# One instruction order for TensorE through a recurrence: products, chain stages and a clock of delays

## The chip, the cores and the metric

The kernel runs on one core of a Trainium2 chip. The metric is the device time of one execution in microseconds (us). Before the change it is 2061.61 us, the median of three runs (2059.32 to 2065.57).

## The reference, cut to what matters

Two layers of a diffusion backbone work on 256 context tokens and 512 latent tokens of width 1024, in float32. The even layer, which comes first, has two token mixers side by side: four mLSTM heads and eight RWKV-7 heads. Their outputs are joined and projected back, and a squared-ReLU MLP of width 4096 follows. The odd layer has RG-LRU and neighbourhood attention in the same places. Context tokens pass through the even layer too, since the odd layer's latent tokens read them.

The change concerns the RWKV-7 mixer. Each head keeps a 64 x 64 state S. Every token decays it, corrects it by a rank-one term and adds another:

```python
def step(S, inp):
    r_t, w_t, k_t, v_t, a_t, b_t = inp
    sa = jnp.einsum('zbhij,zbhj->zbhi', S, a_t)
    S = S * w_t[..., None, :] + sa[..., :, None] * b_t[..., None, :] + v_t[..., :, None] * k_t[..., None, :]
    return S, jnp.einsum('zbhij,zbhj->zbhi', S, r_t)
```

It runs forwards and backwards over the context (256 tokens) and goes on from there over the latent tokens (512). The output is the latent stream after a last normalization.

## The kernel before, in words

**Products.** A float32 product with a weight matrix is made of three products of a rounded type: weight and input are each split into a high and a low part (`split_w` L228 for weights: ScalarE rounds, VectorE or GpSimd subtracts; `split_x` L279 for inputs), and `gemm_w` (L254) sums high x high, high x low and low x high in one PSUM bank. A product of 8 blocks has 24 matmuls, of 512 columns for latent tokens and of 256 for context tokens. Two PSUM banks (`psg`) take turns.

**The recurrence in chunks.** The RWKV scan is cut into 12 steps of 64 tokens (4 context, 8 latent); each step treats both directions and all eight heads. `pre(s)` (L839) prepares a step, independently of the state. Its stages: loads from DRAM (`bk`, `ar`, `AS`, `X`); the products `psA` of 64 rows each, one half of the partitions (`q`) after the other, whose results ScalarE and VectorE mask; a way through DRAM to bring the 16 x 16 blocks of a triangular matrix together (`M`); its inversion in 30 small dependent instructions (`tm`, `Xi`), on GpSimd up to step 4 and on VectorE after it; a way back (`Xr`); and four rounds of tiny matmuls (`psI`), each followed by VectorE or ScalarE, that merge the blocks to the inverse `T`. `step(s)` (L949) is the serial part: `pR` (psC<-X,AS), then `pU` (psC<-r,T), then the new state (psC<-X,BK) and the output (psC<-X,Q and psC<-S,ar), with evictions by ScalarE and VectorE between them. Tiles of a step live in one of two sets of buffers, by `s % 2`.

**What runs between.** `fillers` (L1118) yields the other work of this stage piece by piece: `rwkv_in(1)` (L689), which makes the RWKV inputs of the latent tokens from 15 products and many small operations; half of the output projection for the latent tokens (`lat_mlstm` L1031) and for the context (`ctx_mlstm` L1044); then, when step 3 is done, the other half for the context (`ctx_half` L1058) and the context's whole MLP. `pull` (L1077) takes pieces by their estimated length, and the main loop (L1133) gives `step(s)`, `pre(s+1)` and 21 us of fillers in turn; 33 us of fillers (`PL`) are given ahead of step 0. Steps from 4 on need `rwkv_in(1)` and `lat_mlstm`.

**What sets the order.** The program gives instructions in this order, but each engine's final order is made by a scheduler that simulates the program with a model of durations and puts whatever is ready first. All engines, TensorE too, then run their instructions in that fixed order.

`pre(0)` is given earlier, before the last two pieces of the fourth mLSTM head (string in L1089, letter R).

Of the kernel before, what the change touches and what calls it, by code (L numbers as in the profile page):

```python
# [18 lines left out]
P = 128  # L19
D = 1024  # L20
# [97 lines left out]
def hybrid_kernel(ctx: ExitStack, tc: tile.TileContext, A, out):  # L118
# [12 lines left out]

    def mm(o, l, r, start=True, stop=True, shared=False, tile=None):
        kw = {"tile_position": (32 * tile[0], 32 * tile[1])} if tile else {}
        return nc.tensor.matmul(o, l, r, start=start, stop=stop, skip_group_check=shared, **kw)  # L134
# [93 lines left out]
    def split_w(ap, both, pool=None):  # L228

        m = ap.shape[1]  # L230
        n = m if pool else D
        pool = pool or (wide[0] if wcount[0] % 3 == 2 else None) or wp
        wpool = wide[0] if wide[0] is not None and pool is wide[0] else wp
        w = wpool.tile([P, D], F32, tag="w", bufs=3 if wpool is wp else None, name=nm("w"))[:, 0:m]
        nc.sync.dma_start(w, ap)
        wh = pool.tile([P, n], F32R, tag="wh", name=nm("wh"))[:, 0:m]
        nc.scalar.copy(wh, w)  # L237
        wl = pool.tile([P, n], F32R, tag="wl", name=nm("wl"))[:, 0:m]
        wcount[0] += 1
        eng = nc.vector if (2, 0, 3, 1)[wcount[0] % 4] < both else nc.gpsimd  # L240
        eng.tensor_tensor(wl, w, wh.bitcast(F32), op=ALU.subtract)  # L241
        return wh, wl

    def gemm(ap, xs, psp, both=0, k0=0, k1=NK, x0=0):

        w = split_w(ap[:, P * k0:P * k1], both)
        res = [gemm_w(w, x, psp, x0) for x in xs]
# [6 lines left out]
    def gemm_w(w, x, psp, x0=0):  # L254
        (wh, wl), (xh, xl, n) = w, x
        nk = wh.shape[1] // P
        ps = psp.tile([P, n], F32, tag="g", name=nm("psg"))
        for k in range(nk):
# [97 lines left out]
    def mlp(layer, cnd, n, res, FC, psp, side, both, rb, G, stats=None, done=None):  # L356
        us = n / 512 * 5.2
        with ExitStack() as st:
# [12 lines left out]
            for ch in range(DFF // P // FC):  # L371
# [16 lines left out]
                for m in range(NK // 2 if last and done else NK):  # L388
                    add_gated(res[:, m, :], gemm(A["w2"][layer, ch, m], [(hh, hl, n)], psp, both)[0], cnd, m, layer, 5)
# [299 lines left out]
    def rwkv_in(si, psp, psh, tag, last=None):  # L689
# [5 lines left out]
        with tc.tile_pool(name=nm("pha"), bufs=1) as pha, tc.tile_pool(name=nm("ph"), bufs=1) as ph, \  # L695
# [4 lines left out]
            nc.gpsimd.memset(rst[:, ::CR], 0.0)  # L700
            low = [[pha.tile([P, n], F32R, name=nm("low")) for z in range(2)] for kind in range(2)]
# [26 lines left out]
            for p in range(4):  # L728
                gup = ph.tile([P, P], F32, tag="gup", name=nm("gup"))
                nc.sync.dma_start(gup, A["g_up"][:, P * p:P * p + P])  # L730
                kk, k, r = (ph2.tile([P, nch, 64], F32, tag=a, name=nm(a)) for a in ("kk", "k", "r"))
                v = ph.tile([P, nch, 64], F32, tag="v", name=nm("v"))
                inproj(3 + 3 * p, k)
                sq = pha.tile([P, n], F32, tag="zs", bufs=2, name=nm("sq"))
                nc.scalar.activation(c64(sq), k, AF.Square, scale=V["k_k"][:, p:p + 1])
                pst = psh.tile([P, nb, 2], F32, tag=tag, name=nm("pst"))
                for c in range(nb):
# [7 lines left out]
                               rk.rearrange("p c h -> p (c h)")[:, :, None].to_broadcast([P, 2 * nb, 64]))  # L745
                bc = psh.tile([P, nch, 64], F32, tag=tag, name=nm("psbc"))
# [3 lines left out]
                yield us  # L750
                inproj(4 + 3 * p, r)
                q_ = pha.tile([P, nch, 64], F32, tag="zs", bufs=2, name=nm("q"))
                nc.vector.scalar_tensor_tensor(q_, r, V["r_k"][:, p:p + 1], k, op0=ALU.mult, op1=ALU.mult)
                gb = ph.tile([P, 2, n], F32, tag="gb", name=nm("gb"))
                pb = psh.tile([P, nch, 64], F32, tag=tag, name=nm("psb"))
                mm(pb, C["hsum"], q_)
                nc.scalar.copy(c64(gb[:, 1, :]), pb)
                yield us
                inproj(5 + 3 * p, v)
                if p == 3 and last:  # L760
                    last()
                yield us
                th = []
                for z in range(2):
                    up = ph.tile([P, 2, P], F32, tag="up", name=nm("up"))
                    nc.sync.dma_start(up, A["up"][p, z])
                    uh = ph.tile([P, 2, P], F32R, tag="uh", name=nm("uh"))
                    ul = ph.tile([P, 2, P], F32R, tag="ul", name=nm("ul"))
                    nc.scalar.copy(uh, up)
                    nc.gpsimd.tensor_tensor(ul, up, uh.bitcast(F32), op=ALU.subtract)  # L770
                    for kind in range(2):
                        pw = psh.tile([P, nch, 64], F32, tag=tag, name=nm("psw"))
                        mm(fl(pw), uh[:, kind, :], low[kind][z], True, False)
                        mm(fl(pw), ul[hs_[z], kind, :], low[kind][z][hs_[z], :], False, True)
# [3 lines left out]
                        th.append(t_)  # L778
                for z in range(2):
# [24 lines left out]
                    nc.sync.dma_start(bkD[si][:, st, z, p, :], bk)  # L804
                pv = psh.tile([P, nb, P], F32, tag=tag, name=nm("psv"))
                for c in range(nb):
                    nc.tensor.transpose(pv[:, c, :], fl(v)[:, P * c:P * c + P], ident)
                vt = pha.tile([P, nb, P], F32, tag="zs", bufs=2, name=nm("vt"))
                nc.scalar.copy(vt, pv)
                nc.sync.dma_start(vD[si][:, p, :].rearrange("(c t) i -> t c i", t=P), vt)  # L810
                nc.gpsimd.tensor_tensor(c64(gb[:, 1, :]), c64(gb[:, 1, :]), v, op=ALU.mult)
                pg_ = psh.tile([P, n], F32, tag=tag, name=nm("psg"))
# [4 lines left out]
                yield 0.0  # L817
# [21 lines left out]
    def pre(s, X):  # L839
# [3 lines left out]
        pr2 = sets[s % 2]  # L843
        ar = pr2.tile([P, 2, 4, P], F32, tag="ar", name=nm("ar"))
        bk = pr2.tile([P, 2, 4, P], F32, tag="bk", name=nm("bk"))
        Q = pr2.tile([P, 2, 4, 2, 64], F32, tag="Q", name=nm("Q"))
        AS = pr2.tile([P, 2, 4, 2, 64], F32, tag="AS", name=nm("AS"))
        AB = pr2.tile([P, 2, 4, 64], F32, tag="AB", name=nm("AB"))
# [4 lines left out]
        for z in range(2):  # L853
            c = 64 * (ch[z] - s0)
            nc.sync.dma_start(X[64:P, z].rearrange("t p q i -> t (p q i)"), vD[si][c:c + 64].rearrange("t p i -> t (p i)"))
        for z in range(2):
            for q in range(2):
                pa_ = bank("A", [P, 4, P])
                for p in range(4):
                    mm(pa_[:, p, :], bk[hs_[q], z, p, :], ar[hs_[q], z, p, :])  # L860
                nc.scalar.copy(AB[hs_[q], z], pa_[0:64, :, 0:64])
                nc.vector.tensor_tensor(AS[64:P, z, :, q, :], pa_[64:P, :, 0:64], amask(z, 0, HI), op=ALU.mult)
                nc.vector.tensor_tensor(Q[:, z, :, q, :], pa_[:, :, 64:P], amask(z, 1, FULL), op=ALU.mult)
# [8 lines left out]
        M = pr.tile([64, 16, 16], F32, tag="M", name=nm("M"))  # L872
        Xi = pr.tile([64, 16, 16], F32, tag="Xi", name=nm("Xi"))
        tm = pr.tile([64, 16, 16], F32, tag="tm", name=nm("tm"))
# [6 lines left out]
        for z in range(2):  # L881
            pt = bank("A", [P, 4, P])
            for p in range(4):
                nc.tensor.transpose(pt[:, p, :], bk[:, z, p, :], ident)
# [11 lines left out]
        Xr = pr.tile([P, 8, 32], F32, tag="Xr", name=nm("Xr"))  # L896
        nc.sync.dma_start(Xr, dX.rearrange("u p t -> p u t"))
        Xt = pr.tile([P, 8, 32], F32, tag="Xt", name=nm("Xt"))
        fl8 = lambda a: a.rearrange("p a b -> p (a b)")
        nc.vector.transpose(fl8(Xt), fl8(Xr))  # L900

# [8 lines left out]
        nc.vector.tensor_tensor(dd, pi, lmask, op=ALU.mult)  # L910
        pj = bank("I", [P, 2, 4, 32])
# [11 lines left out]
        for b in range(2):  # L923
            nc.scalar.activation(T[:, :, :, b32[b]], t2, AF.Copy, scale=C["bsel"][:, b:b + 1])
        pi = bank("I", [P, 4, 32])
# [5 lines left out]
        nc.scalar.copy(d1, pi)  # L931
        pj = bank("I", [P, 4, 32])
# [7 lines left out]
        tt = (T[:, 0], T[:, 1])  # L940
        PRE[s] = (ar, GE[:, s], Q, AS, BK, tt)

    PRE = {}
    seen = set()

    def new_x(s):
        return sets[s % 2].tile([P, 2, 4, 2, 64], F32, tag="X", name=nm("X"))

    def step(s, X, S0, Xn):  # L949
# [6 lines left out]
        nc.scalar.copy(r_, pR)  # L956
        pU = bank("C", [P, 2, 4, 64])
# [3 lines left out]
        nc.vector.tensor_copy(X[0:64, :, :, 1, :], pU[64:P])  # L961
        S1 = None
        if s < NCR - 1:
# [3 lines left out]
            S1 = sets[(s + 1) % 2].tile([P, 2, 4, 64], F32, tag="S", name=nm("S"))  # L967
# [23 lines left out]
    def rwkv_norm(y):  # L991
# [7 lines left out]
        sq = sets[0].tile([P, g, u, 64], F32, tag="lv", name=nm("sq"))  # L999
# [14 lines left out]
    def rwkv_gate(si, dst, po, psp):  # L1014

        n = SEGS[si][1]
        for p in range(4):
            gb = po.tile([P, 2, n], F32, tag="gb", name=nm("gb"))
            nc.sync.dma_start(gb, gD[si][:, :, p, :])
            py_ = psp.tile([P, n], F32, tag="g", name=nm("psy"))  # L1020
# [4 lines left out]
            nc.gpsimd.tensor_tensor(dst(p), gb[:, 0], gb[:, 1], op=ALU.add)  # L1025

# [17 lines left out]
    def ctx_mlstm():  # L1044

        pres = st_c.enter_context(tc.tile_pool(name="pres", bufs=1, side="right"))
        res = RES["c"] = pres.tile([P, NK, CT], F32, name="res_c")
        wide[0] = st_w.enter_context(tc.tile_pool(name="wp2", bufs=1, side="right"))
        nc.sync.dma_start(res, xin[:, :, CTX])
        with tc.tile_pool(name="pcm", bufs=1, side="right") as pcm:  # L1050
            xh = pcm.tile([P, 4, CT], F32R, name="xhmc")
            xl = pcm.tile([P, 4, CT], F32R, name="xlmc")
            y = xl.bitcast(F32)
            nc.sync.dma_start(y, moD[:, :, CTX])
            split_x(xh, xl, y)
# [429 lines left out]
```

## Time and profile before

| what | value |
|---|---|
| median of three runs | 2061.61 us |
| the profiled execution, its own time | 2061.51 us |
| its span, first to last instruction | 2059.7 us |
| granted TensorE clock, mean | 0.971 |
| TensorE busy | 1952.0 us, 95% of the span |
| VectorE, ScalarE, GpSimd busy | 1055.2, 875.5, 872.4 us |

The span has 1.8 us less than the execution's time. Busy shares are averages over stages of different kinds: the recurrence lies between about 366 us, when its first preparation starts, and 944 us. The granted clock has two levels, 1.0 (2.4 GHz) and 0.5 (1.2 GHz); a value between them is a mean over both.

### The profile page before, as it was taken

What the parts mean: (1) busy time and instruction counts of PE and PEld (TensorE: products, weight loads), DVE (VectorE), ACT (ScalarE), POOL (GpSimd) and SP (SyncE); (2) the same over time, 40 slices, a digit from 0 to 9 for tenths busy, and PEclk for the clock granted to TensorE, in tenths of its full rate; (3) what the DMA queues carried; (4) which work ended last, traced back from release to release, by engine and by line L of the source; (5) the groups of instructions that cost most, each with busy time, mean ns of one, the idle gap of its engine ahead of it and who ended that gap; (6) DMA issues with size and microseconds to landing.
All of it is one profiled execution on the core that took longest, in us unless ns stands there. A gap on an engine that the chain in (4) does not pass through costs nothing. (4 is left out here: it accounts for less than half of the span.)

```text
span 2059.7 us, 36771 instructions
## 1 busy us (share of the span) xinstructions
PE 1952.0 (95%) x14924; PEld 1604.6 (78%) x14924; DVE 1055.2 (51%) x1944; ACT 875.5 (43%) x1441; POOL 872.4 (42%) x706
## 2 busy tenths in 40 slices
PE   6899998899887999999999999999999999999998
PEld 4788886777677888988787888888666678888887
DVE  6774645676767666766642221353666664122222
ACT  4444444455534443443432332443655654233232
POOL 1455555445534222223244444435444453444444
PEclk9999999999888999999999999999999999999999
DMA  7356557454585555543533323234211122323332
GB/s 301 107 200 214 178 206 262 122 156 124 153 233 143 159 158 156 142 136 124 190 115 125 102 92 103 88 108 153 62 52 34 57 75 82 102 92 101 94 97 78
DMA packets 171833, 271.62 MB, mean 132 GB/s; under 512 B 74960, under 2 KB 113488, under 8 KB 166544
## 3 DMA queue, kind: packets, MB, share of 16 engines
q1 hardware_dynamic: 166608, 263.76, 40.7%
q10 hardware_dynamic: 5056, 5.51, 0.8%
q8 instruction: 118, 1.93, 0.4%
q14 instruction: 51, 0.42, 0.1%
HBM read 244.06 MB, written 25.17 MB: 131 GB/s over the span
## 5 line engine op out<-in xcount | busy, mean ns | idle before, releaser
L241 POOL TENSOR_TENSOR wl<-w,wh 128x1024 fp32r<-128x1024 f32 (+3 forms) x245 | 555.1, 2268 | 829.1 <-PE psg L134 451.9
L237 ACT CAST wh<-w 128x1024 fp32r<-128x1024 f32 (+3 forms) x319 | 313.5, 985 | 543.5 <-PE psg L134 465.1
L134 PE MATMUL psg<-xh,wh 128*128 128x512 f32 (+1 forms) x1440 | 498.2, 361 | 12.8 <-DVE k L710 3.1
L134 PE MATMUL psg<-xl,wh 128*128 128x512 f32 (+1 forms) x1440 | 497.9, 358 | 0.5 <-DVE xl L335 0.4
L134 PEld LDWEIGHTS psg<-xh,wh 128*128 128x128 f32 x1440 | 273.2, 191 | 68.0 <-issue 16.9
L134 PE MATMUL psg<-xh,wl 128*128 128x512 f32 (+1 forms) x1440 | 325.3, 356 | 0.0
L134 PEld LDWEIGHTS psg<-xl,wh 128*128 128x128 f32 x1440 | 275.4, 191 | 45.0 <-issue 7.2
L134 PEld LDWEIGHTS psg<-xh,wl 128*128 128x128 f32 x1440 | 241.9, 190 | 42.1 <-issue 7.3
L134 PE MATMUL psg<-hh,wh 128*128 128x512 f32 (+1 forms) x800 | 266.9, 350 | 6.2 <-DVE r L383 3.2
L134 PE MATMUL psg<-hl,wh 128*128 128x512 f32 (+1 forms) x800 | 268.8, 350 | 0.9 <-DVE hl L281 0.8
L338 DVE SCALAR_TENSOR_TENSOR res_l<-psg,mod,res_l 128x512 f32<-128x512 f32 (+1 forms) x108 | 74.2, 689 | 276.3 <-PE psg L134 276.2
L134 PEld LDWEIGHTS psg<-hh,wh 128*128 128x128 f32 x800 | 151.9, 190 | 27.6 <-issue 4.2
L134 PEld LDWEIGHTS psg<-hl,wh 128*128 128x128 f32 x800 | 152.1, 190 | 20.6 <-DVE hl L281 1.2
L134 PE MATMUL psg<-hh,wl 128*128 128x512 f32 (+1 forms) x800 | 166.4, 350 | 0.0
L134 PEld LDWEIGHTS psg<-hh,wl 128*128 128x128 f32 x800 | 132.9, 191 | 19.2
L383 DVE TENSOR_SCALAR r<-psg 128x512 f32<-128x512 f32 (+1 forms) x96 | 57.4, 600 | 171.4 <-PE psg L134 171.2
L281 DVE TENSOR_TENSOR hl<-r,hh 128x512 fp32r<-128x512 f32 (+1 forms) x96 | 86.8, 907 | 80.4 <-ACT hh L280 80.4
L384 ACT ACTIVATE r<-r 128x512 f32<-128x512 f32 (+1 forms) x96 | 53.5, 560 | 125.8 <-DVE r L383 125.8
L241 DVE TENSOR_TENSOR wl<-w,wh 128x1024 fp32r<-128x1024 f32 (+1 forms) x74 | 88.1, 1191 | 34.9 <-ACT wh L237 15.5
L134 PE MATMUL psada<-adaw,sc 128*32 128x256 f32 (+1 forms) x896 | 62.4, 383 | 7.7 <-DMA adaw<-in_ada_w_dram 4.1
L134 PE MATMUL psA<-ar,bk 64*128 64x128 f32 x384 | 51.5, 295 | 7.3 <-issue 3.0
L280 ACT CAST hh<-r 128x512 fp32r<-128x512 f32 (+1 forms) x96 | 52.6, 550 | 2.8
(422 smaller groups left out, 2900.5 us busy)
## 6 DMA issues: line engine op xcount, KB each, us to landing
w<-in_w_dram SPq DMA_DIRECT2D x192, 512.0 KB, 3.5
adaw<-in_ada_w_dram SPq DMA_DIRECT2D x40, 1024.0 KB, 7.5
w<-in_ev_in_dram SPq DMA_DIRECT2D x47, 512.0 KB, 3.5
w<-in_od_in_dram SPq DMA_DIRECT2D x32, 512.0 KB, 3.5
adaw<-in_ada_dram SPq DMA_DIRECT2D x16, 512.0 KB, 10.8
w<-in_out_w_dram SPq DMA_DIRECT2D x32, 256.0 KB, 2.9
bk<-bkD SPq DMA_DIRECT2D x12, 512.0 KB, 4.7
ar<-arD SPq DMA_DIRECT2D x12, 512.0 KB, 5.7
```

What stands on the lines that cost most here:

```text
L134: return nc.tensor.matmul(o, l, r, start=start, stop=stop, skip_group_check=shared, **kw)
L237: nc.scalar.copy(wh, w)
L241: eng.tensor_tensor(wl, w, wh.bitcast(F32), op=ALU.subtract)
L280: nc.scalar.copy(h, x)
L281: nc.vector.tensor_tensor(l, x, h.bitcast(F32), op=ALU.subtract)
L338: nc.vector.scalar_tensor_tensor(r_, ps, modcol(layer, idx, m, cnd), r_, op0=ALU.mult, op1=ALU.add)
L383: nc.vector.tensor_scalar(r_, ps, 0.0, None, op0=ALU.max)
L384: nc.scalar.activation(r_, r_, AF.Square)
```

## The change

TensorE's instructions in the recurrence stage are no longer placed by the scheduler: inside a marked region they keep the order in which the program gives them. The program makes that order with a clock `now`, which advances with the columns of each matmul given. After each matmul, `poll` looks at five queues of generators and gives the next stage of each one that is due. A stage ends in `yield d`, d us on that clock, or in `yield` of a condition. The other engines are still placed by the scheduler.

```diff
+    now, ordered, queues = [0.0], [False, False], {k: [] for k in ("step", "odd", "even", "in", "gate")}
+    def poll():
...
+            q = next((q for q in queues.values() if q and due(q[0])), None)
+            if q:
+                d = next(q[0][0], None)
...
+                    q[0][1] = d if callable(d) else now[0] + d
...
     def mm(o, l, r, start=True, stop=True, shared=False, tile=None):
...
+        if ordered[0]:
+            n = math.prod(r.shape[1:])
+            now[0] += n * (1.0 if r.dtype == F32R else 4.0) / 2260 * (0.5 if l.shape[0] <= 64 else 1.0)
+            poll()
```

`settle(cond)` moves the clock on to the next due time, without products, until a condition holds.

`pre` becomes `front` and `back`. In `front`, the two halves of `psA` alternate wherever two banks are there (from step 1 on):

```diff
+        yield 13.0 if s == CT // CR else 9.0
...
+            for heads in (((0, 1),) if banks["A"][2] > 1 else ((0,), (1,))):
...
                 for p in range(4):
-                    mm(pa_[:, p, :], bk[hs_[q], z, p, :], ar[hs_[q], z, p, :])
...
+                    for q in heads:
+                        mm(pa_[q][:, p, :], bk[hs_[q], z, p, :], ar[hs_[q], z, p, :])
...
+            yield 3.0
```

`back` yields 33.0 after it has given the inversion and the way through DRAM, and 1.4, 2.4, 1.2 and 2.0 after the four `psI` rounds. `step` yields 1.5 after `pR` and 2.0 after `pU`, and the chain 3.6 after each step. Steps use three sets of buffers, and up to two preparations run at once:

```diff
+    set_of = lambda s: sets[(0, 1, 0, 1, 0, 2, 1, 0, 2, 1, 0, 2)[s]]
...
+        return steps[0] >= s - (1 if s <= CT // CR else 2) and (s < CT // CR or "in" in done)
...
+    def chain(S):
+        for s in range(NCR):
+            yield lambda: s in PRE and (s < CT // CR or "lat" in done)
+            S = yield from step(s, new_x(s), S, new_x(s + 1) if s + 1 < NCR else None)
+            rwkv_norms(s)
+            steps[0] = s + 1
+            yield 3.6
```

The main loop goes; `pre(0)` is given as before, without regard to its yields, and then:

```diff
-    PL = [18, 15, 21, 10, 21]
-    pull(fill, PL[0])
-    for s in range(NCR):
...
+    ordered[0] = True
+    with tc.manual_schedule(engines={mybir.EngineType.PE}):
+        queues["step"].append([chain(S), 0.0])
+        queues["odd"].append([prepare(1), 0.0])
+        queues["even"].append([prepare(0), 0.0])
+        for _ in fill:
+            if steps[0] == NCR and "ctx" in done:
+                break
+        settle(lambda: steps[0] == NCR)
```

In `rwkv_in`, the small operations of a head pair become a generator `operands` with yields of 1.2 to 4.2 (nine TensorE stages for each of four pairs), spawned after the first of the pair's three products. The low part of its weights is multiplied over 128 rows instead of 64. Fillers are rearranged: the loads and first four products of `lat_mlstm` come inside `rwkv_in` as its tail; `ctx_parts` makes the loads of both context halves ahead of their products, and the gate becomes a stage of its own queue. In the MLP of the context, the first two products of the first layer run together, block by block (`G` 0 to 2). The first product of the MLP's second layer takes its last block last:

```diff
+        if late:
+            for k0, k1 in ((0, nk - 1), (nk - 1, nk)):
+                for w_, x_ in ((wh, xh), (wh, xl), (wl, xh)):
+                    for k in range(k0, k1):
+                        mm(ps, w_[:, P * k:P * k + P], x_[:, x0 + k, :], k == 0 and x_ is xh and w_ is wh, k == nk - 1 and w_ is wl)
```

The raw weights no longer have a fourth buffer while the context's products run, and the normalization's squares share the buffer `r` with the step.

## Rows read from the trace of the kernel before

**Rows 1.** The page, parts 1 and 2: busy time; granted clock in 40 slices.
```profile
PE 1952.0 (95%) x14924; PEld 1604.6 (78%) x14924; DVE 1055.2 (51%) x1944; ACT 875.5 (43%) x1441; POOL 872.4 (42%) x706
...
PEclk9999999999888999999999999999999999999999
```
**Rows 2.** Busy time by windows: stretch, length, each engine, PEclk, DMA share, GB/s.
```profile
390.00:421.00 31.00, 28.22 (x254) 22.90 (x253) 18.59 (x28) 14.78 (x22) 12.46 (x29) 1.00 0.36 106
400.00:600.00 200.00, 182.57 (x2056) 139.90 (x2054) 133.84 (x220) 98.10 (x173) 94.21 (x166) 0.91 0.56 157
600.00:700.00 100.00, 82.87 (x1197) 76.94 (x1198) 69.37 (x169) 45.84 (x90) 30.34 (x48) 0.86 0.58 159
400.00:1000.00 600.00, 549.07 (x7147) 479.67 (x7146) 401.69 (x831) 269.99 (x469) 213.16 (x266) 0.94 0.53 151
```
**Rows 3.** Waits of TensorE, 385 to 1000 us: total us, times, longest.
```profile
PE psI L134 <- DMA Xr<-invD: 7.8, 6, 3.0
PE psg L134 <- DVE res_c L338: 5.6, 3, 2.8
PE psg L134 <- DVE gb L1024: 4.7, 1, 4.7
PE psg L134 <- ACT xhom L280: 4.6, 1, 4.6
PE psg L134 <- DVE r L383: 3.2, 3, 1.7
PE psg L134 <- DVE k L710: 3.1, 2, 1.9
```
**Rows 4.** Timeline of TensorE, 380 to 431 us: start, us, instruction, idle before.
```profile
385.13 0.58 PE L134 MATMUL psg<-xh,wh 128*128 128x512 f32 x1 [2.78 <-DVE dn L664]
...
408.13 0.28 PE L134 MATMUL pst<-cst,sq 128*128 128x2 f32 x2
409.02 0.45 PE L134 MATMUL psI<-Xr,AB 32*32 32x32 f32 x32 [0.62 <-DMA Xr<-invD]
...
430.17 1.03 PE L134 MATMUL psC<-X,AS 128*64 128x64 f32 x26
```
**Rows 5.** Timeline of TensorE: stages that prepare step 3 (first row) and step 5.
```profile
565.88 0.48 PE L134 MATMUL psI<-Xr,dd 32*32 32x32 f32 x32
...
623.32 1.71 PE L134 MATMUL psA<-ar,bk 64*128 64x128 f32 x16
...
672.04 0.45 PE L134 MATMUL psI<-Xr,AB 32*32 32x32 f32 x32 [1.11 <-DMA Xr<-invD]
...
682.51 0.45 PE L134 MATMUL psI<-t,d 32*32 32x32 f32 x32
```
**Rows 6.** Timeline of VectorE: its answers to two of these stages.
```profile
572.54 0.41 DVE L920 STREAM_TRANSPOSE t<-t 128x256 f32<-128x256 f32 x1
...
683.69 0.60 DVE L939 SCALAR_TENSOR_TENSOR T<-psI,cst,T 128x128 f32<-128x128 f32 x2
```
**Rows 7.** TensorE groups by form, 400 to 1000 us: busy, mean ns, idle before.
```profile
L134 PE MATMUL psA<-ar,bk 64*128 64x128 f32 x352 | 45.6, 292 | 4.3 <-DVE ms L997 2.8 <-DVE Q L863 0.8 <-DMA bk<-bkD 0.7
L134 PE MATMUL psC<-r,T 64*64 64x64 f32 x384 | 15.4, 237 | 1.2 <-DVE T L939 1.2
```
**Rows 8.** Timeline of TensorE: a stage between products; the last of 106 such changes.
```profile
737.27 0.28 PE L134 MATMUL psg<-hl,wh 128*128 128x256 f32 x1
737.39 0.28 PE L134 MATMUL psg<-hh,wh 128*128 128x256 f32 x1
737.60 0.33 PE L134 MATMUL psC<-X,BK 128*64 128x64 f32 x2
737.86 0.39 PE L134 MATMUL psg<-hl,wh 128*128 128x256 f32 x1
738.08 0.28 PE L134 MATMUL psg<-hh,wh 128*128 128x256 f32 x1
...
956.23 2.31 PE L134 MATMUL psy<-cst,ya_l 64*64 64x64 f32 x70
```

## The prediction before the run

> **What bounds the kernel now.** I read the busy shares first. TensorE is busy for 1952.0 of 2059.7 us, so a gain must come out of its 107.7 idle us, out of time at its lower clock, or out of its own work; the slices of the clock show where it falls [rows 1]. The windows come next: 400 to 1000 us, the stretch of the recurrence, has 549.07 us of work in 600, so 50.9 us idle, nearly half of all. Its mean clock is 0.94; with the two levels 2.4 and 1.2 GHz, 12% of the stretch (72 us) was at the lower one, which costs 36 us, or 33 once the part in which TensorE stood idle anyway is taken off. The worst hundred us, 600 to 700, have 17.1 us idle and a clock of 0.86 [rows 2]. So some 84 us are lost here. Then the waits: the longest sum is for the inverted blocks that come back from DRAM, 7.8 us in six times, and the next are products that wait for an eviction or a freshly made input (5.6, 4.7, 4.6, 3.2, 3.1 us) [rows 3]. None is long: the scheduler's order is wrong by a little in many places.
>
> The sum is made against the profiled execution's own 2061.5 us (its span and 1.8 us), which is the median of the runs (2061.6).
>
> **Waits of products.** The change aims at most of them: loads of the projection's inputs ahead of need (4.6), the gate as a stage of its own (4.7), a last block last (3.2), delays in place of a modelled time for the return from DRAM (7.2 of the 7.8 lie after 400 us). Of the 50.9 us I keep 8: the 3.1 for `k`, half of the 5.6 for `res_c`, and 2 for all others [rows 2, 3]. Bounds 4 and 14.
>
> **Stages given too early.** TensorE runs in order, so a stage whose input isn't ready now stops the products behind it, and whoever waits for those: ScalarE's and VectorE's evictions and the weight buffers. The delays are fixed, while VectorE is 67 to 69% busy from 400 to 700 us [rows 2]. Two rows bound what happens. The second merge round for step 3 started last at 565.88; its answer ended at 572.54 + 0.41 = 572.95, 7.1 us later, against a delay of 2.4. The last round for step 5 started at 682.51 and was answered by 683.69 + 0.60 = 684.29, 1.8 us later, against 2.0 [rows 5, 6]. A stall per step is thus between 0 and 4.7 us, if one of a step's rounds meets it; over 12 steps 0 to 56 us. I take 1.8 a step, 22 us: nearer the short end, since only steps 1 to 3 now run beside the dense VectorE work of `rwkv_in`. The long delay is safer: from the start of the last `psA` for step 5 (623.32 + 1.71 = 625.03 at its end) to the first merge (672.04) 47 us passed [rows 5], against 3.0 + 1 for transposes + 33 = 37 on the new clock. So that one could still be 10 us late; it is in the 22.
>
> Idle in the stretch without the next part: 8 + 22 = 30, 21 less than before.
>
> **The start.** Before, 33 us of products come ahead of step 0. Now step 0 is in its queue, due at 0.0, and `PRE[0]` is there as far as the program knows; `pR` goes after the first matmul and `pU` 1.5 us later, behind some eight matmuls. But `pU` needs step 0's `T`. The inverse came back at 409.02 [rows 4], by a way through GpSimd and DRAM that TensorE's order doesn't shorten; four merge rounds, without products between them, take what step 5's took, 684.29 - 672.04 = 12.3 us [rows 5, 6]. So `T` is there at 421, while TensorE had its first product at 385.13 [rows 4] and eight matmuls and `pR` last until about 390. Between 390 and 421 TensorE was busy for 28.2 us [rows 2]; about 2.6 of it, the last transposes of head 3 and two merge rounds, stay. The other 25.6, products, move behind the wait: +26. Nothing covers it, as all mLSTM work is over. Bounds: 0, if `T` is early or the order isn't strict, and 31.
>
> The Trainium skill's page TensorE: Matmul & The Clock Gate (Step-by-step: what each phase is for) says that matmuls stay in program order and only weight loads are pulled ahead. By that rule the hole stands; if later matmuls could pass, the sum would be the first rival's. No run here shows a matmul that passes another.
>
> **The clock.** Less idle time means less time at 1.2 GHz, but a hole of 30 us brings its own. I scale 33 us with the idle time outside the hole (30 of 51: 19): -14. Bounds -28 (with 8 us idle) and +5.
>
> **`psA` in alternating halves.** 352 matmuls (22 groups of 16) take 45.6 us, 2.07 a group. `pU` has the same columns per group (32 of 64 instead of 16 of 128) and alternates the halves: 15.4 / 12 = 1.28 [rows 7]. 22 x 0.79 = -17. Bounds -22 and -8, as `pU`'s group also differs in width.
>
> **More changes between products and stages.** From 737.39 to 738.08 stand two products' pitches and a pair of 64 columns: 0.69 - 2 x 0.11 - 0.08 (a sixteenth of 1.28) = 0.39 us is the price of going there and back; 0.11 is 256 columns at the 2260 a us of the change's clock [rows 8]. In the trace TensorE leaves products 106 times between 408.13 and 956.23 [rows 4, 8]. By the code there are 3 stages a step, 7 a preparation and 9 for each of four pairs: 36 + 77 + 36, with the gate and statistics some 157. Those due together go together. +4, bounds 0 and 51 x 0.39 = 20.
>
> The Trainium skill's page TensorEngine Tiling (Array Packing) (Key Properties) has TensorE drain when the tiling mode changes, which speaks against more changes. The trace agrees as far as the 0.39 us go; with all 157 paid, the sum would be 16 us higher.
>
> **What is moved or added at no cost.** The loads of a preparation (six issues on SP) come earlier and stand in front of weight loads; SP's queue stops if a set isn't free, and then weights wait. Three sets and three weight buffers, each worth a product of 24 x 0.11 = 2.7 us or more, hide that; if the cover goes, up to 2.7 us a step, 32. The normalization's squares and the step share `r`: the next `pR`'s copy waits for the squares' sum, which is at most four times and hidden by 3.6 us and more. 128 rows instead of 64 stream the same columns: 0. Inversions up to step 4 stay on GpSimd, 35% busy in the stretch [rows 2]; its weight splits stand behind them as before.
>
> Does the recurrence get slower than its fillers? On the new clock a preparation takes 9 + 6 + 33 + 7 and some 7 of matmuls, 62, and two run at once: 31 a step. `rwkv_in` ends near 145 and the last step near 425. Fillers and recurrence together have (products at 2260 columns a us: 82 + 22 + 22 + 174, small ones 20, recurrence 145) 465. So products outlast the chain, and what is left runs after it as before.
>
> **The sum.** 2061.5 - 21 + 26 - 14 - 17 + 4 = 2039.5; predicted 2040.
>
> **Rivals.**
> The first step isn't held up: `T` comes early, or the region lets products pass. For it: such a hole is plain in any profile of this order. Against it: nothing in the code delays step 0. 2040 - 26 - 2 of clock = 2012.
> Slower: the delays are too short for a busy VectorE. Place: the in-order TensorE at the 113 stages of steps and preparations. If each step pays one wait like that at 572.95, stalls are 56 instead of 22; the pairs' 36 stages at 0.3 us add 11, and then the clock gains nothing (+14 against the sum): 2040 + 34 + 11 + 14 = 2099. It decides when the stalls pass 22 + 20 = 42 us, 3.5 a step, and lies mostly at 2070 to 2100. For it: the first row of [rows 5] and its answer, and that steps follow each other at 31 instead of about 43 us (515 us from 430 [rows 4] to the last, over 12), so that VectorE's share rises. Against it: the last round for step 5, answered in time [rows 5, 6].
> No change: hole and new stalls eat the gain; 2061.
>
> **How the numbers follow.** Forecast 0.45 (its own range 2022 to 2060), first rival 0.25, slower rival 0.22, no change 0.08. The range 1992 to 2088 takes in most of the first rival, whose best end (no hole, 12 us idle, clock -26, `psA` -17) is 2061.5 - 39 - 26 - 17 = 1980, and half of the slow one's span. About 0.3%, 6 us, is what a measurement can tell from no change: below 2055 lie 0.36 of the forecast, all of the first rival and a little more: 0.62. Within 6 us: 0.06 of the forecast, most of the no-change case: 0.13. Slower: 0.25.
>
> **What would show it.** An idle gap of about 30 us before the first psC<-r,T; without it the start was wrong. Groups of `psA` at 1.3 us. Idle from the hole's end to 1000 us of about 30, most of it ended by VectorE in front of `psI` and `psC`; if it is over 50, the delays were wrong. A mean clock in the stretch of 0.96 or more. The last step well before 944 us and context products after it. A time below 2000 or above 2075 would make the sum wrong.

## The result and the profile after

The changed kernel takes 2114.7 us (median of four runs, 2113.2 to 2116.5) beside 2063.1 for the kernel before on the same chip: ratio 1.025, 95% interval 1.023 to 1.027. That is 75 us above the prediction and outside its range. The profiled execution has a span of 2111.3 us, 51.6 more than before.

The page, parts 1 and 2 (busy time; granted clock in 40 slices), answers to [rows 1].

```profile
PE 1932.4 (92%) x14924; PEld 1591.6 (75%) x14924; DVE 1079.3 (51%) x1947; ACT 874.6 (41%) x1444; POOL 869.4 (41%) x706
...
PEclk9999998698988898999999999999999999999999
```

TensorE's work fell by 19.6 us (1952.0 to 1932.4) and its idle time rose from 107.7 to 2111.3 - 1932.4 = 178.9, by 71.2. The difference is the loss: 71.2 - 19.6 = 51.6. So on balance the loss is idle time, and the windows say where: first the kernel before, 200 to 400 us; then the changed kernel, with the stretches of [rows 2].

```profile
200.00:400.00 200.00, 187.32 (x1305) 149.53 (x1305) 114.83 (x260) 89.02 (x181) 103.06 (x114) 0.96 0.58 195
```

```profile
200.00:400.00 200.00, 160.99 (x1225) 129.93 (x1227) 102.07 (x250) 82.86 (x173) 101.39 (x129) 0.89 0.57 187
390.00:421.00 31.00, 18.34 (x391) 15.39 (x392) 6.04 (x14) 5.33 (x11) 3.89 (x14) 0.64 0.19 44
400.00:600.00 200.00, 167.26 (x1899) 129.69 (x1890) 135.50 (x206) 93.89 (x163) 82.42 (x142) 0.88 0.43 125
600.00:700.00 100.00, 73.21 (x590) 61.89 (x590) 61.70 (x140) 37.94 (x73) 37.99 (x53) 0.85 0.64 185
400.00:1000.00 600.00, 506.89 (x6845) 441.74 (x6837) 404.00 (x801) 255.91 (x451) 191.01 (x233) 0.90 0.49 142
```

From 200 to 400 us, 39.0 us are idle instead of 12.7 (+26.3). From 400 to 1000 us, 93.1 instead of 50.9 (+42.2). All the rest differs by 2.7. The clock in the second stretch fell from 0.94 to 0.90.

The start, in TensorE's timeline (start, us, instruction, idle before): where [rows 4] had products from 385.13 on, all four merge rounds of step 0 now stand ahead of the first product, and the first of them waits 16.51 us for the inverse from DRAM.

```profile
381.66 1.54 PE L736 MATMUL pst<-cst,hall 128*128 128x128 f32 x6 [2.27 <-POOL hall L731]
399.71 0.65 PE L172 MATMUL psI<-Xr,AB 32*32 32x32 f32 x32 [16.51 <-DMA Xr<-invD]
...
406.18 1.97 PE L172 MATMUL psC<-X,AS 128*64 128x64 f32 x32 [0.84 <-PE psI L172]
408.08 0.80 PE L172 MATMUL psg<-xl,wh 128*128 128x512 f32 x1
```

So the hole lasts from 381.66 + 1.54 = 383.2 to 408. The windows ahead of it and of it, first in the kernel before, then in the changed one:

```profile
200.00:383.20 183.20, 173.56 (x1249) 138.49 (x1248) 100.37 (x240) 79.35 (x166) 89.18 (x89) 0.96 0.58 199
383.20:408.00 24.80, 21.77 (x91) 17.65 (x92) 16.83 (x24) 11.64 (x19) 16.16 (x34) 0.93 0.50 134
```
```profile
200.00:383.20 183.20, 160.70 (x1205) 129.64 (x1203) 101.08 (x248) 82.13 (x171) 92.11 (x96) 0.93 0.60 198
383.20:408.00 24.80, 5.34 (x225) 4.82 (x224) 3.10 (x8) 1.90 (x5) 9.28 (x34) 0.50 0.19 51
```

The hole has 16.4 us more idle time than the same stretch had before (19.5 instead of 3.0), and the stretch ahead of it 12.9 more (22.5 instead of 9.6).

TensorE's waits, 385 to 1000 us (total us, times, longest), answer to [rows 3]. The names have changed: `dd`, `X`, `t` and `r` are answers to stages of the recurrence, `th` and `rx` answers to the operands' stages, and the products' waits for `res_c` grew from 5.6 to 9.4.

```profile
PE psI L172 <- DMA Xr<-invD: 16.5, 1, 16.5
PE psI L172 <- DVE dd L1018: 11.0, 5, 3.8
PE psg L172 <- DVE res_c L391: 9.4, 7, 2.1
PE psw L172 <- ACT th L825: 8.7, 3, 7.2
PE psC L172 <- ACT r L1083: 8.5, 3, 5.8
PE psC L172 <- DVE X L1089: 8.2, 4, 3.7
PE psg L172 <- DVE y L385: 6.5, 1, 6.5
PE psbc L172 <- ACT rx L808: 5.6, 2, 5.2
PE psI L172 <- DVE t L1029: 4.7, 3, 3.3
```

The groups by form, 400 to 1000 us, answer to [rows 7]: `psA` takes 26.4 us instead of 45.6.

```profile
L172 PE MATMUL psA<-ar,bk 64*128 64x128 f32 x352 | 26.4, 285 | 2.6 <-DVE Q L964 2.6
L172 PE MATMUL psC<-r,T 64*64 64x64 f32 x384 | 15.2, 235 | 8.5 <-ACT r L1083 8.5
```

### The profile page after: what moved, and what is told of

The parts are those of the page before. It is cut to its first block, busy times and chain, and to the rows that moved or that the text cites. A ratio compares the mean times of both kernels' runs of the same rounds, so it can differ in the third digit from the quotient of the medians.

```text
span 2111.3 us, 36782 instructions
## 1 busy us (share of the span) xinstructions
PE 1932.4 (92%) x14924; PEld 1591.6 (75%) x14924; DVE 1079.3 (51%) x1947; ACT 874.6 (41%) x1444; POOL 869.4 (41%) x706
## 5 line engine op out<-in xcount | busy, mean ns | idle before, releaser
L172 PE MATMUL psg<-xh,wh 128*128 128x512 f32 (+1 forms) x1440 | 504.3, 364 | 18.6 <-DVE y L385 6.5
L172 PE MATMUL psg<-xl,wh 128*128 128x512 f32 (+1 forms) x1440 | 506.1, 363 | 0.8 <-DVE xl L388 0.7
L172 PE MATMUL psg<-xh,wl 128*128 128x512 f32 (+1 forms) x1440 | 331.8, 358 | 0.0
L172 PEld LDWEIGHTS psg<-xl,wh 128*128 128x128 f32 x1440 | 279.5, 194 | 46.5 <-issue 7.3
L334 DVE TENSOR_TENSOR hl<-r,hh 128x512 fp32r<-128x512 f32 (+1 forms) x96 | 93.1, 974 | 86.2 <-ACT hh L333 86.0
L287 DVE TENSOR_TENSOR wl<-w,wh 128x1024 fp32r<-128x1024 f32 (+1 forms) x74 | 93.4, 1262 | 29.5 <-ACT wh L283 23.4
L995 POOL TENSOR_TENSOR tm<-M,Xi 64x15 f32<-64x15 f32 (+7 forms) x75 | 26.9, 358 | 62.4 <-DMA M<-dA 57.5
```

What stands on the lines that cost most here:

```text
L172: ins = nc.tensor.matmul(o, l, r, start=start, stop=stop, skip_group_check=shared, **kw)
L334: nc.vector.tensor_tensor(l, x, h.bitcast(F32), op=ALU.subtract)
L995: eng.tensor_tensor(t_, M[:, m:16, j:j + 1].to_broadcast([64, n, m]), Xi[:, j:j + 1, 0:m].to_broadcast([64, n, m]), op=ALU.mult)
```

## The experiments

Theory "order": the loss comes from holding TensorE to the emission order. Rival "load": VectorE and ScalarE answer late whatever the order. Each ratio below is to the kernel before, run beside it; 0.001 is 2.06 us.

**No region** (ratio 1.0050, 1.0031 to 1.0070; 2071.7 us).
```diff
-    with tc.manual_schedule(engines={mybir.EngineType.PE}):
+    if True:
```


> The changed kernel without its TensorE region: the program is emitted in the same order, with the same sets, delays, operand generator and loads, but the scheduler places TensorE's instructions as in the kernel before. Theory 'order' (the time is lost because TensorE, held to the emission order, stands at stages whose answers are late, 41 us more idle between 420 and 1000 us, and at the first step, 28 us more idle between 200 and 420): both go, 2114.7 - 41 - 28 = 2046 (2030 to 2065). Rival 'load' (VectorE and ScalarE answer late whatever the order, because two preparations, the steps and the operands now press on them at once): only the start's idle time goes, 2114.7 - 28 = 2087 (2078 to 2100).


Between the two: 2.0% better, but still slower than before. Its busy time and windows:

```profile
PE 1928.5 (93%) x14924; PEld 1588.7 (77%) x14924; DVE 1075.8 (52%) x1947; ACT 872.0 (42%) x1444; POOL 876.0 (42%) x706
```
```profile
200.00:400.00 200.00, 188.17 (x1338) 152.75 (x1338) 120.68 (x270) 95.56 (x193) 97.60 (x110) 0.97 0.59 194
400.00:1000.00 600.00, 513.77 (x7052) 450.75 (x7051) 408.85 (x817) 253.84 (x454) 216.13 (x264) 0.92 0.52 147
```

The start's idle time is gone (11.8 us from 200 to 400); from 400 to 1000 us 86.2 remain. The strict order made the hole; of the 42.2 us later on only 7 went with it. Over the whole span 2071.7 - 1928.5 = 143.2 us are idle, 35.7 fewer than in the changed kernel and 35.5 more than in the kernel before: about half of the new idle time goes with the region, and half stays.

**The start mended** (1.0149, 1.0121 to 1.0177; 2092.7).
```diff
-            for _ in back(0):
-                pass
+            back0 = back(0)
+            next(back0)
...
-        queues["even"].append([prepare(0), 0.0])
+        queues["even"].append([itertools.chain(back0, prepare(0)), 24.0])
```


> The changed kernel, but the merge rounds of step 0 stand in the 'even' queue and fall due 24 us of the clock after the first product, instead of being emitted ahead of all products; step 0 waits for them in its queue. Theory 'order': the 28 us of idle time between 200 and 420 go, some at the lower clock with them: 2114.7 - 28 - 4 = 2083 (2075 to 2092). If the start is not where the order costs (TensorE would have had nothing ready to run there anyway): 2105 to 2116.


1.0% (21 us) came back; 21.6 us stay idle from 200 to 400, against 12.7 before.

**`psA` alone, in the kernel before** (0.9981, 0.9964 to 0.9998; 2056.3), in `pre`:
```diff
-            for q in range(2):
-                pa_ = bank("A", [P, 4, P])
+            pa_ = [None, None]
+            for heads in (((0, 1),) if banks["A"][2] > 1 else ((0,), (1,))):
+                for q in heads:
+                    pa_[q] = bank("A", [P, 4, P])
                 for p in range(4):
-                    mm(pa_[:, p, :], bk[hs_[q], z, p, :], ar[hs_[q], z, p, :])
+                    for q in heads:
+                        mm(pa_[q][:, p, :], bk[hs_[q], z, p, :], ar[hs_[q], z, p, :])
...
```


> The kernel before with one part of the change alone: the products psA of both heads alternate between the halves of the array. By the sum of the prediction 22 groups x 0.79 us = 17 us of TensorE's work go: 2063 - 17 = 2046 (2041 to 2055). Rival: the scheduler of the kernel before sets the halves apart again, or the saved work turns into waits for evictions: 2058 to 2066.


The rival was right: a ratio of 0.9981 is 4 us, not 17. The scheduler pulls many of the groups apart again: `psA` costs 42.8 us in the whole trace, against 51.5 before and 31.3 in the changed kernel. Part of the saved work also turns into waits: idle time from 420 to 1000 us rises from 49 to 55 us.

What holds VectorE up? In the changed kernel, VectorE's timeline behind the merge round that ended at 786.51 + 0.48 = 786.99, and then GpSimd's and TensorE's:

```profile
787.53 1.22 DVE L287 TENSOR_TENSOR wl<-w,wh 128x1024 fp32r<-128x1024 f32 x1
788.78 0.20 DVE L997 TENSOR_TENSOR Xi<-Xi,tm 64x39 f32<-64x39 f32 x1
...
789.47 2.33 DVE L995 TENSOR_TENSOR tm<-M,Xi 64x28 f32<-64x28 f32 x1
...
792.05 0.42 DVE L1018 TENSOR_TENSOR dd<-psI,cst 128x256 f32<-128x256 f32 x1
```
```profile
789.41 2.34 POOL L287 TENSOR_TENSOR wl<-w,wh 128x1024 fp32r<-128x1024 f32 x1 [4.63 <-ACT wh L283]
```
```profile
786.51 0.48 PE L172 MATMUL psI<-Xt,AB 32*32 32x32 f32 x32
...
792.53 0.65 PE L172 MATMUL psI<-Xt,dd 32*32 32x32 f32 x32 [3.79 <-DVE dd L1018]
```

`dd` ended 5.5 us after its round, against a delay of 1.4. Ahead of it stood a weight split and the other preparation's inversion, of which one operation took 2.33 us instead of 0.2.

Late answers are not new, and the usual answer is no slower. Of the 12 answers `dd` in the changed kernel eight ended within 1.2 us of their round and four after 4.8 to 5.5; in the kernel before eleven ended within 2.3 and one after 5.8. VectorE's half of `X` ended 1.4 to 6.3 us after its round, with a median of 2.3; before it was 1.4 to 6.0 and 2.2. In the kernel before the one late `dd` cost no wait, as the scheduler had put products between the two rounds (VectorE's timeline, then TensorE's):

```profile
415.32 0.41 DVE L910 TENSOR_TENSOR dd<-psI,cst 128x256 f32<-128x256 f32 x1
```
```profile
409.50 0.45 PE L134 MATMUL psI<-Xt,AB 32*32 32x32 f32 x32
...
415.81 0.39 PE L134 MATMUL psg<-xh,wh 128*128 128x512 f32 x1
416.13 0.45 PE L134 MATMUL psI<-Xt,dd 32*32 32x32 f32 x32
```

So the delay of 1.4 fits the usual `dd` and misses the late ones; the 2.0 for `X` lies a little below its median. With the start mended VectorE also stood still, 6.39 us, at a transfer from DRAM, ahead of an `X` for which TensorE then waited 5.64:

```profile
524.44 0.45 DVE L1005 STREAM_TRANSPOSE Xt<-Xr 128x256 f32<-128x256 f32 x1 [6.39 <-DMA Xr<-invD]
524.92 0.69 DVE L1089 COPY X<-psC 64x512 f32<-64x512 f32 x1
```

So the next runs set "queue" (what stands in front of an answer on VectorE) against "delays" (too short as a rule). All start from the mended start.

**Late VectorE work** (1.0200, 1.0174 to 1.0225; 2098.8).
```diff
+        keys[0] = s
+        yield 9.0
         eng = nc.gpsimd if s <= CT // CR else nc.vector
...
+        yield 24.0
         nc.vector.transpose(fl8(Xt), fl8(Xr))
-        keys[0] = s
-        yield 33.0
+        yield 0.6
```


> The kernel with the start mended (2092.7 us; 420 to 1000 us: 95 us idle, of which 31 are waits of stages for X and dd), and with what VectorE does for the inversion emitted later: its 30 operations 9 us of the clock after the loads of M are issued, the transposes Xt after the long delay (24 after the operations, so 33 in all as before) instead of ahead of it. Theory 'queue' (VectorE takes its work in order, and in front of X, dd and the evictions stand operations that wait for M or Xr from DRAM: 6.4 us for Xr ahead of the X that ended at 525.6, 4.6 us for M ahead of the X that ended at 899.8): waits for X and dd fall from 31 to 10 us and some of the 14 for res_c go, 2092.7 - 24 = 2069 (2058 to 2080). Rival 'delays' (1.4 and 2.0 us are simply shorter than an answer takes): 2086 to 2098.


A miss for "queue": waits for `X` and `dd` fell from 31 to 16 us, but others grew (the MLP's `r` from 2.6 to 8.5, `t` from 0.2 to 8.5); in all 96 us are idle from 420 to 1000, and it was 95 without the edit.

**Inversions on GpSimd** (1.0065, 1.0040 to 1.0090; 2070.6).
```diff
-        eng = nc.gpsimd if s <= CT // CR else nc.vector
+        eng = nc.gpsimd
```


> The kernel with the start mended, and with the inversions of all steps on GpSimd (before: those of steps 5 to 11 on VectorE). Theory 'queue', in its second form (the 30 operations of an inversion, 11 to 21 us on VectorE, stand in front of X and dd of the other preparation): the waits for dd (9.9 us) and the three for X after 700 us (14 us) mostly go, 2092.7 - 18 = 2075 (2064 to 2084). Rival 'delays': nothing changes, 2086 to 2098; it is slower if GpSimd's weight splits wl come late behind 13 us of inversion.


As "queue" expected: 0.84% (17 us).

**Longer short delays** (1.0080, 1.0054 to 1.0106; 2073.3).
```diff
-                    q[0][1] = d if callable(d) else now[0] + d
+                    q[0][1] = d if callable(d) else now[0] + d + (1.0 if d < 5 else 0.0)
...
-        yield 33.0
+        yield 24.0
```


> The kernel with the start mended, with 1.0 us added to every delay below 5 us, and the long delay cut from 33 to 24 us so that the fillers still outlast the chain. Theory 'queue' (single waits for dd and X last 3 to 6.5 us): each of some 20 waits shrinks by 1 us, 2092.7 - 12 = 2081 (2072 to 2088). Rival 'delays' (answers take 1 us more than the delay as a rule): 2092.7 - 30 = 2063 (2052 to 2071).


14 us came back, in the range of "queue". The long delay was changed with the short ones, so the 14 us can't be put down to one of them. Short delays longer by 2.0 us were not measured.

**Late VectorE work without the region** (both diffs; 1.0069, 1.0043 to 1.0094; 2072.1).


> The late emission of the inversion's VectorE operations, as in the run before, but without the TensorE region (2071.7 us without the late emission; 420 to 1000 us: 83 us idle, of which stages wait for Xr 10.9, dd 7.0, T 7.0, X 9.3). Theory 'queue': the order of VectorE costs here too, T, dd and X lose 15 of 23 us: 2071.7 - 15 = 2057 (2046 to 2064). If the strict order is what counts and not VectorE's queue: 2066 to 2076.


No gain over the first run; yet with the region the same program is 1.3% (27 us) slower.

**Together**: GpSimd's inversions and the longer short delays as above, and late transposes (1.0086, 1.0052 to 1.0120; 2079.4); then late inversions too (1.0070, 1.0042 to 1.0098; 2076.6).
```diff
+        keys[0] = s
+        yield 24.0
         nc.vector.transpose(fl8(Xt), fl8(Xr))
-        keys[0] = s
-        yield 33.0
+        yield 0.6
```
```diff
+        keys[0] = s
+        yield 7.0
         eng = nc.gpsimd
...
+        yield 14.0
         nc.vector.transpose(fl8(Xt), fl8(Xr))
```


> The mended start, all inversions on GpSimd, 1.0 us more on every delay below 5 us, and the transposes Xt emitted after the long delay (24) instead of ahead of it. Theory 'queue': the two parts tried alone add up (2092.7 - 22 - 19.5 = 2051), and VectorE no longer stands at the return of Xr (10.7 and 7.9 us ahead of two evictions of res_c, for which TensorE waited 6.2 and 3.4 us): another 12, 2039 (2030 to 2052). Rival 'delays' (the two parts took the same waits away twice): 2062 to 2072.

> As the run with late transposes, and the 30 operations of the inversion emitted 7 us of the clock after the loads of M (then 14 to the transposes), so that GpSimd's weight splits need not stand behind M (8.8 us of GpSimd's idle time ahead of an inversion after 700 us). Theory 'queue': GpSimd's splits come earlier, 2 to 8 us better than without it: 2034 (2026 to 2050). Rival: GpSimd has time enough and the later inversion makes the merge wait: 2045 to 2065.


Both miss "queue", and are slower than their rivals' ranges too. Nothing adds up. The waits of the first of them, 420 to 1000 us:

```profile
PE psA L180 <- DVE Q L964: 17.9, 6, 7.0
PE psg L172 <- DVE res_c L391: 7.5, 4, 4.4
PE psI L172 <- DVE t L1030: 7.4, 2, 4.2
```

`X` and `dd` have all but left the list (0 and 1.4, after 20.8 and 9.9 with the start mended alone), and `Q` (6.3 there) and `t` (0.2 there) have taken their place.

**The first of these without the region** (0.9972, 0.9954 to 0.9990; 2053.2).


> As the run with late transposes, without the TensorE region. If the region's strict order costs nothing once VectorE's queue is in order: within 6 us of that run. If the strict order has a price of its own: 10 us or more faster than that run. If the order by hand is worth something: 10 us or more slower.


One edit, 1.14% (24 us): the strict order has a price of its own, and without it this version has the lowest ratio of all. It is faster than both kernels, if only by 0.3% beside the kernel before; three other versions lie within its interval.

**Control: the kernel before with all inversions on GpSimd** (1.0046, 1.0030 to 1.0061; 2070.7).


> A control: the kernel before, with the inversions of all steps on GpSimd and nothing else. If the collision of inversion and answers on VectorE is something that the change brought (pairs of preparations side by side, TensorE held to its order): 2059 within 5 us. If it is worth as much in the kernel before (22 us), it is no part of what the change lost: 2035 to 2045.


It (the diff on `eng`) gets slower by 0.5% (10 us), more than either theory gave, where the same edit gave the changed kernel with its start mended 17 us. So the gain of this edit is particular to the changed kernel. That the kernel before loses nothing to inversions on VectorE isn't shown, since GpSimd's own load has a price too, which no run separates.

**GpSimd's inversions and longer delays, with the region** (1.0072, 1.0050 to 1.0094; 2075.5).


> The mended start, all inversions on GpSimd, 1.0 us more on every delay below 5 us, the long delay 24; the transposes Xt where the change has them. If the two parts take different waits away: 2092.7 - 22 - 19.5 = 2051 (2044 to 2058), and the late transposes cost 28 us in the run that had them. If both take the same waits away: 2066 to 2074, the price of the strict order that delays of this kind leave.


They took the same waits away, as the two together gain no more than each alone; the late transposes did not cost the 28 us (this version and the one that had them differ by 3).

**No region, GpSimd's inversions, late transposes, delays as in the change** (0.9983, 0.9965 to 1.0001; 2055.5); **without late transposes** (1.0033, 1.0013 to 1.0052; 2066.4).


> No TensorE region, mended start, all inversions on GpSimd, Xt emitted after the long delay (33), the short delays as in the change. Theory 'queue' (VectorE's load is what stays of the loss without the region): 2053 to 2060, as with longer delays (2053). Rival (the delays set the emission order and so the priorities, and it was these that helped): 2066 to 2074, as without the region alone (2071.7).

> No TensorE region, mended start, all inversions on GpSimd; transposes and delays as in the change. If the inversions on VectorE are what stays of the loss: 2054 to 2060, as with late transposes (2055.5). If the early transposes, for which VectorE waits on DRAM, are it: 2066 to 2073.


The transposes are worth 0.5% (10 us) here, the longer delays nothing that can be told. VectorE's waits at DRAM, 400 to 1000 us, first without the region alone, then in the fastest version:

```profile
DVE Xt L1005 <- DMA Xr<-invD: 48.1, 11, 8.2
DVE tm L995 <- DMA M<-dA: 19.2, 6, 8.0
```
```profile
DVE Xt L1007 <- DMA Xr<-invD: 41.6, 11, 8.4
```

67.3 us have become 41.6, by three edits: the 19.2 for `tm` went with the inversions to GpSimd, and the late transposes alone took the wait for `Xr` from 52.7 to 45.6 (the last pair of runs). The kernel before has 33.7 + 12.8 = 46.5, the changed one 52.3 + 18.5 = 70.8.

**Two other edits undone** (first chunk's group of two, last block last): without the region alone 1.0040 (1.0025 to 1.0055), in the fastest version 0.9978 (0.9962 to 0.9994).
```diff
-                    add_gated(res[:, m, :], gemm(A["w2"][layer, ch, m], [(hh, hl, n)], psp, both, late=ordered[0] and m == 0)[0], cnd, m, layer, 5)
+                    add_gated(res[:, m, :], gemm(A["w2"][layer, ch, m], [(hh, hl, n)], psp, both)[0], cnd, m, layer, 5)
...
-        yield from mlp(0, 1, CT, res, 8, psg2, "right", WS[3], rb, 2)
+        yield from mlp(0, 1, CT, res, 8, psg2, "right", WS[3], rb, 0)
```


> No TensorE region and nothing else mended (2071.7), but two of the other edits undone: the context mlp's first chunk without the group of two, and the first product of the second matrix without its last block last. If these edits cost what stays of the loss: 2059 to 2065. If not: 2069 to 2076.

> The fastest run so far (no region, mended start, inversions on GpSimd, late transposes, 1.0 us longer delays: 2053.2) with the group of two and the last block last undone as well. If the 4 us that these gave alone add up: 2049 (2044 to 2052), faster than both kernels by 0.4% or more. If they took the same waits away: 2052 to 2055.


Neither differs from its partner beyond the intervals; these edits are not where the time went.

## Why the prediction was wrong

The sum had idle time up by 5 us (-21 in the stretch from 400 to 1000, +26 at the start) and work down by 27 (clock, `psA`, changes). Measured were +71.2 and -19.6. Nearly the whole miss is idle time in the stretch: 93 us, where 8 + 22 = 30 were forecast. On balance all other terms are off by some 10.

**Right: the kind and place of the start.** A hole was forecast with +26, and 21 us came back when it was mended. But it began earlier (383) and ended earlier (408) than worked out: the merge rounds, given ahead of the region, held up the products, and not `pU` behind eight of them; and the inverse was back at 399.7 and not 409, since GpSimd had ended the inversion at 394.1 and not at 402.4. The hole itself has +16.4; the other 12.9 lie ahead of it, from 200 to 383, where nothing was forecast. That 200 to 400 us have +26.3 in all is luck. The rule of the Trainium skill's page TensorE: Matmul & The Clock Gate (Step-by-step: what each phase is for), that matmuls stay in program order, agrees with this trace: 16.51 us passed with products emitted behind.

**Right: `psA`.** -17 forecast, 51.5 - 31.3 = -20.2. The strict order gives the whole of it; without the region the program's order still gives most (37.0 us without the region, 39.1 in the fastest version).

**Wrong sign, small: the changes between products and stages.** +4 forecast. TensorE does leave products more often (123 times between 408 and 1000 us, before 105), but its stages now run whole: the `psC` matmuls stand in 68 pieces instead of 116. The six groups of `psC` and of transposes `psA<-cst,bk` fell from 102.5 to 90.3 us in the trace; those of `psI` rose by 2.6. -10.

**Wrong: "Of the 50.9 us I keep 8".** By the list of waits from 420 to 1000 us products waited 27 us before and 25 after. I had ascribed these waits to loads and order on TensorE. But 18 of the 25 end with an answer of VectorE (`res_c` 9.4, `y` 6.5), and 6 with one of ScalarE. Three of the waits for `res_c`, 5.7 us together, end behind a slowed operation of an inversion, as here:

```profile
947.56 2.30 DVE L995 TENSOR_TENSOR tm<-M,Xi 64x60 f32<-64x60 f32 x1
...
950.65 0.48 DVE L391 SCALAR_TENSOR_TENSOR res_c<-psg,mod,res_c 128x256 f32<-128x256 f32 x1
```
```profile
951.28 0.35 PE L172 MATMUL psg<-hh,wh 128*128 128x256 f32 x1 [2.02 <-DVE res_c L391]
```

For `y` VectorE makes eight blocks one after another, with 2.2 us of an inversion between them; that explains only a part of its 6.5.

**Wrong: "Stages given too early", 22.** This is the step that failed by most. Stages of steps and preparations waited 36 us after 420 us (17 before). The operands' stages, moved into a queue of their own, waited another 21 (1 before), and gate and statistics 9 (4): I had counted none of the last two. Together 66, not 22. The prediction took 1.8 us of stall a step, between a late and a punctual answer of the kernel before. The usual answers `dd` and `X` take about the time they took there (medians 0.8 and 2.3 us, before 1.3 and 2.2), but in the held order nothing else runs in the time of the late ones. By the prediction's own sign (over 50 us idle after the hole; there are 90 from 408 to 1000) the delays were wrong. My slower rival had the place, and nearly the price of stalls (56 + 11), but not its parts: steps and preparations 36 instead of 56, the pairs 21 instead of 11. That the sum fits is luck. Its decision point, 42, was passed, and the time lies 16 us above its 2099.

**Wrong: the clock.** -14 forecast. By the trace's records of the granted clock 115 us of the stretch were at 1.2 GHz (75 before), and in 89 of them TensorE worked (68 before). At half speed that is 45 us lost instead of 34, so +10 (an estimate from these figures). It shows in the work: `psA` and the stages took off 20 + 10 us, and 19.6 are left.

**Wrong: the pace.** The last step began at 986.5 us, later than before (926.4), with pairs some 80 us apart. Most of the delay arises at one place: from step 3 to step 4 125 us pass (597.3 to 722.6; before 59.8), as the preparation of step 4 can start only when `rwkv_in(1)` is done, at 641.8 (before 594.8), and its merge begins 70 us later (before 48). The program's clock counts only columns, so waits and the lower clock stretch it as well.

Shown: the region costs time. In the changed kernel as it is, it costs 42 us of the 52 (1.0252 to 1.0050), half of it the hole (21 by the mended start). In three versions with the start mended it costs 7, 24 and 27 us (pairs with that one edit: 1.0065 to 1.0033, 1.0086 to 0.9972, 1.0200 to 1.0069; the first is within its uncertainty). With the region, the inversions on VectorE cost 17. These are not additive: under the region five repairs of queue or delays end at 2071 to 2079 and a sixth at 2099; where one answer comes in time, TensorE waits at the next. The 10 us that stay without the region go with the inversions on GpSimd and the late transposes together (1.0050 to 0.9983, 10 us of it by the transposes); whether late transposes would help the kernel before too was not measured. The region's price varies with the version, and which waits make up the difference is not settled. Nor is why the clock stays at 0.92 in the fastest version, where only 65.6 us are idle (600 - 534.43).

## What to carry to other kernels

A hand-written order on one engine is only as good as the longest queue of the engines that answer: before giving an order to TensorE, list for each answer what else is on VectorE's and ScalarE's queues then, above all what waits for DRAM there. A fixed delay can fit the usual answer and still miss the late ones (here four of 12 `dd`); an order that is held pays for each of these, where a looser one has other work in between. A prologue that was hidden by reordering must be put into the new order as well.

## What the runs showed of the hardware

A small operation on VectorE can last as long as one on GpSimd. Of the 210 operations of inversions on VectorE (0.2 us each) 12 took 1.5 to 2.3 us in the changed kernel, and each of the 12 ended within 0.1 us after a weight split on GpSimd ended (as 789.47 + 2.33 = 791.80 and 789.41 + 2.34 = 791.75): 26 us of VectorE in all, 23 more than at 0.2 each. The kernel before has 14 such operations, 30 us, so they are not what the change brought. The Trainium skill's page SBUF — State Buffer (Who interferes with whom) says that a VectorE instruction with two inputs in SBUF contends with a GpSimd instruction that reads SBUF; the trace agrees: all 12 have two inputs in SBUF, and so has the weight split.
